# Both gates as one product of 2x2 blocks in seven block products, with sigmoids in DRAM and a merge stage of its own

## The chip, the cores and the metric

The kernel runs on one core of a Trainium2 chip. The metric is device microseconds of one execution; several runs are given by their median. The engines of the core work in parallel, each in the order of its own queue, and wait for one another by semaphores: PE (TensorE, matrix products and transposes), DVE (VectorE), ACT (ScalarE), POOL (GpSimd, which here also issues DMAs that store to DRAM) and SP (SyncE, which here issues the DMA loads).

## The reference

One decoder block on x of 1024 tokens and 1024 channels, all in float32. The part that matters here:

```python
h = rmsnorm(x, norm1_g[l])
proj = h @ w_in[l]
...
gate_a = jax.nn.sigmoid(proj[..., QKV_COLS + 2 * SGU_WIDTH:QKV_COLS + 2 * SGU_WIDTH + D_MODEL])
gate_b = jax.nn.sigmoid(proj[..., QKV_COLS + 2 * SGU_WIDTH + D_MODEL:])
...
sgu = spatial_gating(uv, sgu_ln_g[l], sgu_ln_b[l], w_spatial[l], b_spatial[l])

merged = gate_a * (attn @ w_proj_attn[l]) + gate_b * (sgu @ w_proj_sgu[l])
x = x + merged @ w_out[l]

h2 = rmsnorm(x, norm2_g[l])
ff = jax.nn.silu(h2 @ w_ffn_gate[l]) * (h2 @ w_ffn_up[l])
x = x + ff @ w_ffn_down[l]
```

Each gate is 1024 tokens x 1024 columns with 1024 summed; attn and sgu have 512 channels. `spatial_gating` applies Gelu to u and v, a layer norm to v, mixes v over 128 tokens with a triangular matrix for each of 8 groups, and multiplies by u.

## The kernel before

**Numbers.** A float32 matrix is kept as a pair of float32r: `split` (L102) writes the high part with a CAST on ACT (L103) and the rest with a subtraction on DVE (L104). A product of two such pairs is three matmuls (high x high, high x low, low x high), each 128 summed x 128 x 512 columns. H holds h, transposed, as 2 x 8 blocks of 128 channels x 1024 tokens.

**Stages.** RMSNorm to H; attention in four rounds (hp), whose result goes to DRAM as attd (tile tag "att", L588 to L593); the SGU stage with v and then u (eight token tiles T each, `rows_mm`, L363 to L365, Gelu L771); the gate stage (L818 on); the out product with W_o, which adds x (L1033); the FFN (`product`, L990 to L992, 22 column blocks); the down product; the last RMSNorm.

**The SGU's end.** After every second T of u, `mix` (products L739, and L743 on DVE with scalar_tensor_tensor) and `sgu_T` (four transposes for each T, L753, then four small splits of 128x128) are put into a table of slots: `at(slot, f)` runs f when PE's program has come to that slot, so the last ones fall among the gate products.

**The gate stage.** For ph 0 (gate_b and sgu) and ph 1 (gate_a and attention), for each of 8 column blocks c, and for each half of the tokens: `gate(half)` is 24 matmuls into "acc" (`cols_mm`, L376 to L378) and a Sigmoid (L828) into an SBUF tile "S"; `proj(half)` is 12 matmuls into "s", and DVE multiplies (L836; L838 and L839 add in ph 1) into the merged tile. In all 1152 matmuls. After the last column the 16 halves of merged are split into H.

**What sets the order.** Weights come through a queue of jobs: SP loads into a ring of three "raw" buffers, and `split_job` splits into a ring of 4096 columns, WH and WL. `combine_wd` (L807 to L812, one for each of 11 row pairs of w_ffn_down) forms differences of blocks on DVE for the down product; POOL loads (L801) and stores them (L812). A scheduler lays the program out, and each engine then runs its own instructions in the order laid down.

**The FFN's seven products.** With the four blocks of the weights b11, b21 (gate columns, lower and upper half of the sum) and b12, b22 (up columns), and of H (`OPS`; sums of blocks in HX), four results are made of seven block products instead of eight (Strassen and Winograd's form). `weights(f, i)` (L956 on) splits one block or a difference of blocks, five products ahead (AHEAD_W); `product(f, i)` multiplies.

## Time and profile before

| what | us |
|---|---|
| median of three runs (1715.13 to 1716.87) | 1716.21 |
| the profiled execution, its own time | 1713.07 |
| its span in the trace | 1711.4 |
| last product of u starts | 689.65 |
| first gate product starts | 690.02 |
| first add of x in the out stage | 964.62 |

The profile is of one execution. Its span runs from the first instruction to the last; some 1.7 us of the execution's time lie outside. A busy share is an average over stages with different limits, so the stage that is changed is read by its own windows. In a row of the timeline the first number is the start, the second the duration, then engine, line of the kernel, operation, out<-in; in brackets the engine's idle time before it and what ended that. An entry of the DMA list ends with the median time from issue to landing.

### The profile page before, as it was taken

The numbers are of one execution on the slowest core, as the hardware profiler recorded it, in microseconds if no ns is written. First come the engines' busy times: TensorE is split into PE (matmuls) and PEld (weight loads), VectorE is DVE, ScalarE is ACT, GpSimd is POOL, SyncE is SP. The second block draws the span as 40 slices with busy tenths as digits, with TensorE's granted clock in tenths as the row PEclk, the third lists the DMA queues.
The fourth block names the chain that finished last, engine by engine and source line by source line (L and its number), as shares of the span: only waits on it lengthen the run. The fifth ranks groups of instructions, "written<-read, shape, count | busy, mean of one in ns | idle before, by whom it ended". The sixth has DMA issues, their size and how long they took to land.

```text
span 1711.4 us, 22153 instructions
## 1 busy us (share of the span) xinstructions
PE 1679.3 (98%) x8206; PEld 1363.4 (80%) x8206; DVE 918.3 (54%) x1751; ACT 667.7 (39%) x1319; POOL 203.9 (12%) x361
## 2 busy tenths in 40 slices
PE   7999999999999999999999998999999999989998
PEld 7877877877887778888888886888888888778886
DVE  5355376357447655543323438565565555565555
ACT  5344435425434552311311226333333333354444
POOL 6200120030021124120000011010000000100003
PEclk9999999999999999999999998999999999999999
DMA  7312331152241215763311323233332332397563
GB/s 215 90 43 68 86 100 48 33 151 56 54 139 45 57 27 179 240 235 134 103 45 58 139 74 123 68 119 104 109 100 93 99 102 71 134 355 238 191 194 111
DMA packets 185740, 198.17 MB, mean 116 GB/s; under 512 B 13280, under 2 KB 140640, under 8 KB 185632
## 3 DMA queue, kind: packets, MB, share of 16 engines
q1 hardware_dynamic: 152656, 129.01, 24.3%
q0 software_dynamic: 17616, 58.31, 9.9%
q10 hardware_dynamic: 15360, 9.45, 2.3%
q8 instruction: 64, 1.05, 0.3%
q14 instruction: 44, 0.36, 0.1%
HBM read 144.84 MB, written 48.73 MB: 113 GB/s over the span
## 4 chain that ended last, share of the span: by engine, by line
PE 48%; issue 24%; POOL 2%; DVE 1%; DMA 1%; ACT 1%; SPq 0%; POOLq 0%; ACTq 0%; DVEq 0%
PE ps_acc L376 5%; PE ps_acc L377 5%; PE ps_acc L378 5%; PE ps_acc L364 4%; PE ps_acc L363 4%; PE ps_acc L365 4%; PE ps_dX L1116 2%; PE ps_dX L1117 2%; PE ps_dX L1118 2%; PE ps_s L377 2%; PE ps_s L378 2%; PE ps_s L376 2%; PE ps_s L463 2%; PE ps_dV L1118 1%; PE ps_dV L1116 1%
## 5 line engine op out<-in xcount | busy, mean ns | idle before, releaser
L103 ACT CAST WH<-raw 128x512 fp32r<-128x512 f32 (+2 forms) x179 | 138.5, 776 | 309.4 <-PE ps_acc L377 84.4
L376 PE MATMUL ps_acc<-H,WH 128*128 128x512 f32 x640 | 253.7, 396 | 0.0
L378 PE MATMUL ps_acc<-H,WL 128*128 128x512 f32 x640 | 253.2, 396 | 0.0
L377 PE MATMUL ps_acc<-H,WH 128*128 128x512 f32 x640 | 252.8, 395 | 0.0
L104 DVE TENSOR_TENSOR WL<-raw,WH 128x512 fp32r<-128x512 f32 (+2 forms) x179 | 157.0, 878 | 97.7 <-ACT WH L103 97.1
L363 PE MATMUL ps_acc<-WH,H 128*128 128x384 f32 (+1 forms) x512 | 190.9, 375 | 2.4 <-ACT H L103 2.4
L365 PE MATMUL ps_acc<-WH,H 128*128 128x384 f32 (+1 forms) x512 | 190.8, 373 | 0.5 <-DVE H L104 0.5
L364 PE MATMUL ps_acc<-WL,H 128*128 128x384 f32 (+1 forms) x512 | 189.2, 371 | 0.0
L376 PEld LDWEIGHTS ps_acc<-H,WH 128*128 128x128 f32 x640 | 120.2, 188 | 26.9 <-issue 1.2
L378 PEld LDWEIGHTS ps_acc<-H,WL 128*128 128x128 f32 x640 | 120.3, 188 | 26.8 <-issue 0.3
L377 PEld LDWEIGHTS ps_acc<-H,WH 128*128 128x128 f32 x640 | 120.2, 188 | 25.9 <-issue 0.5
L481 ACT ACTIVATE S<-S,sm 128x128 f32<-128x128 f32 (+1 forms) x192 | 84.9, 444 | 80.6 <-DVE sm L479 74.7
L363 PEld LDWEIGHTS ps_acc<-WH,H 128*128 128x128 f32 x512 | 97.1, 190 | 15.0 <-ACT H L103 2.9
L365 PEld LDWEIGHTS ps_acc<-WH,H 128*128 128x128 f32 x512 | 97.3, 190 | 12.8 <-issue 1.0
L364 PEld LDWEIGHTS ps_acc<-WL,H 128*128 128x128 f32 x512 | 96.8, 189 | 11.5 <-DVE WL L104 0.4
L990 PE MATMUL ps_X<-H,WH 128*128 128x512 f32 x264 | 104.5, 396 | 0.7 <-ACT sn L995 0.7
L991 PE MATMUL ps_X<-H,WH 128*128 128x512 f32 x264 | 104.5, 396 | 0.0
L992 PE MATMUL ps_X<-H,WL 128*128 128x512 f32 x264 | 101.0, 393 | 0.0
L104 DVE TENSOR_TENSOR WL<-rows,WH 128x512 fp32r<-128x512 f32 x66 | 45.4, 691 | 89.8 <-ACT WH L103 89.8
L103 ACT CAST WH<-rows 128x512 fp32r<-128x512 f32 x66 | 40.7, 622 | 129.9 <-PE ps_X L991 92.0
L104 DVE TENSOR_TENSOR WL<-ab,WH 128x512 fp32r<-128x512 f32 x74 | 51.1, 691 | 59.1 <-ACT WH L103 59.1
L103 ACT CAST WH<-ab 128x512 fp32r<-128x512 f32 x74 | 46.0, 621 | 76.3 <-PE ps_dV L1117 40.7
(292 smaller groups left out, 3240.7 us busy)
## 6 DMA issues: line engine op xcount, KB each, us to landing
raw<-in_w_in_dram SPq DMA_DIRECT2D x48, 512.0 KB
att<-in_w_ffn_down_dram POOLq DMA_DIRECT2D x22, 512.0 KB, 4.7
twd<-att POOLq DMA_DIRECT2D x22, 512.0 KB, 3.3
rows<-in_w_ffn_gate_dram SPq DMA_DIRECT2D x22, 512.0 KB
rows<-in_w_ffn_up_dram SPq DMA_DIRECT2D x22, 512.0 KB
ab<-twd SPq DMA_DIRECT2D x44, 256.0 KB
ab<-in_w_ffn_down_dram SPq DMA_DIRECT2D x30, 256.0 KB
raw<-in_w_in_dram SPq DMA_DIRECT2D x32, 192.0 KB
```

The costliest lines, as they stand in the source:

```text
L103: nc.scalar.copy(hi, src)
L104: return tt(out=lo, in0=src, in1=fb(hi), op=ALU.subtract)
L363: mm(o, H[:, 0, kt, tok], wh, start=(kt == 0), stop=False)
L364: mm(o, H[:, 0, kt, tok], wl, start=False, stop=False)
L365: mm(o, H[:, 1, kt, tok], wh, start=False, stop=(kt == KT - 1))
L376: mm(ps, WH[:, w], rh[:, half_of(half)], start=(kt == 0), stop=False)
L377: mm(ps, WH[:, w], rl[:, half_of(half)], start=False, stop=False)
L378: mm(ps, WL[:, w], rh[:, half_of(half)], start=False, stop=(kt == n - 1))
L481: nc.scalar.activation(sbt[:, o:o + n], sbt[:, o:o + n], AF.Exp, bias=neg[:, i:i + 1], scale=0.125, accum_out=stt[:, b, 2 + h:3 + h])
L990: mm(ps, WH[:, w], OPS[i](0, k), start=first and k == 0, stop=False, skip_group_check=True)
L991: mm(ps, WH[:, w], OPS[i](1, k), start=False, stop=False, skip_group_check=True)
L992: mm(ps, WL[:, w], OPS[i](0, k), start=False, stop=k == 3, skip_group_check=True)
```

## The change

The gate stage is replaced by two stages. In the first, gate_a and gate_b are one product of h with [gate_a | gate_b]: for each of 8 column blocks c, seven block products of 12 matmuls, with the functions `weights` and `product` that the FFN had (now made by `seven`, used by both). Their results are sigmoids of 128 x 1024, which POOL stores to gates_d. In the second, "merge", sgu and attention are loaded from DRAM (sgud, attd), split, multiplied by the projection weights, and multiplied by the sigmoids, loaded back from gates_d.

For the block sums of h, `combine_h1(T)` is called in u's T = 1 to 4 (for T - 1): eight adds on DVE and four stores of 256 KB to s7d. Before the gate stage the sums are loaded back and split into HX and into half of H. `sgu_T` no longer splits: one copy on ACT and one store to sgud. The table of slots is emptied before the gate stage (the loop over `sched`), and the pools of the first stages are closed, so nothing of the SGU runs among the gate products. `combine_wd` runs once for each c of the gate stage and three times in the merge. Splits are as before, but stand one line on (L104, L105), and so do other lines.

```diff
-            split(sguT[i][0][:, tok_of(T)], sguT[i][1][:, tok_of(T)], ps[:, i * P:(i + 1) * P])
+        t = T_("vst", [P, 4, P])
+        nc.scalar.copy(t.rearrange("p i t -> p (i t)"), ps)
+        nc.gpsimd.dma_start(out=sgud[:, :, tok_of(T)], in_=t)
...
+    def combine_h1(T):
+        a, b = tok_of(T), tok_of(T + 4)
+        x0, x1 = (T_("att", [P, 2, 4, P]) for _ in range(2))
+        for t, tok in ((x0, b), (x1, a)):
+            for j, kk in enumerate((LO, HI)):
+                tt(out=t[:, j], in0=fb(H[:, 0, kk, tok]), in1=fb(H[:, 1, kk, tok]), op=ALU.add)
+        tt(out=x0[:, 1], in0=x0[:, 0], in1=x0[:, 1], op=ALU.add)
+        tt(out=x0[:, 0], in0=x1[:, 0], in1=x0[:, 0], op=ALU.subtract)
+        tt(out=x1[:, 0], in0=x0[:, 1], in1=x1[:, 0], op=ALU.subtract)
+        tt(out=x1[:, 1], in0=x1[:, 1], in1=x1[:, 0], op=ALU.subtract)
+        for i, t in enumerate((x0, x1)):
+            for j in range(2):
+                nc.gpsimd.dma_start(out=s7d[i][j][:, :, a], in_=t[:, j])
...
+            if 1 <= T < 5:
+                combine_h1(T - 1)
...
+    for n in sorted(sched):
+        for f in sched.pop(n):
+            f()
+    close_pool(first_pool)
+    close_pool(first_psum)
...
+        def keep(f, i, src):
+            a = ring[0] % 8 * 512
+            ring[0] += 1
+            marks["lo"] = split(WH[:, a:a + 512], WL[:, a:a + 512], src)
+            slots[f, i] = a
+        def weights(f, i):
+            g, u = raw[f]
+            b11, b21, b12, b22 = flat(g[:, LO]), flat(g[:, HI]), flat(u[:, LO]), flat(u[:, HI])
+            if i in (1, 2, 3):
+                return keep(f, i, {1: b11, 2: b21, 3: b22}[i])
+            if i == 6:
+                t2 = T_("raw", [P, 512])
+                ts[f] = {5: b11, 6: t2, 7: b12, 4: b21}
+                for o, p, q in ((b11, b12, b11), (t2, b22, b11), (b12, b22, b12), (b21, b21, t2)):
+                    tt(out=o, in0=p, in1=q, op=ALU.subtract)
+            keep(f, i, ts[f][i])
...
+            ps, a = acc[f, b], slots.pop((f, i))
+            for k in range(4):
+                w = slice(a + k * P, a + (k + 1) * P)
+                mm(ps, WH[:, w], OPS[i](0, k), start=first and k == 0, stop=False, skip_group_check=True)
+                mm(ps, WH[:, w], OPS[i](1, k), start=False, stop=False, skip_group_check=True)
+                mm(ps, WL[:, w], OPS[i](0, k), start=False, stop=k == 3, skip_group_check=True)
+            if i in (1, 6, 7):
+                snap[f, i] = T_("sn", [P, 512])
+                nc.scalar.copy(snap[f, i], ps)
+            after(f, i, ps, acc.get((f, "V")), snap, f == nf - 1)
...
+    def gates_after(c, i, ps, V, snap, last):
+        sig = lambda o, src: nc.scalar.activation(o, src, AF.Sigmoid)
+        if i == 2:
+            o = go[c, 0] = T_("go", [P, S])
+            tt(out=o[:, t0], in0=snap.pop((c, 1)), in1=ps, op=ALU.add)
+            sig(o[:, t0], o[:, t0])
+        if i == 7:
+            o = go[c, 1] = T_("go", [P, S])
+            tt(out=o[:, t1], in0=snap.pop((c, 7)), in1=V, op=ALU.add)
+            sig(o[:, t1], o[:, t1])
+            if last:
+                tt(out=o[:, t0], in0=snap[c, 6], in1=V, op=ALU.add)
+            combine_wd(c)
+            load_wd(c + 1, "raw") if c + 1 < KT else None
+        if i == 4:
+            sig(go[c, 0][:, t1], ps)
+            put(gates_d[0][c], go.pop((c, 0)))
+        if i == 3:
+            o = go.pop((c, 1))
+            tt(out=o[:, t0], in0=o[:, t0] if last else snap[c, 6], in1=ps, op=ALU.add)
+            sig(o[:, t0], o[:, t0])
+            put(gates_d[1][c], o)
...
+    for n in range(5):
+        weights(*order[n])
+    with tc.issue_after(marks["load"].ins), tc.issue_after(marks["hi"].ins), tc.issue_after(marks["lo"].ins):
+        for i, j, dst in ((1, 0, 1), (0, 1, 0), (0, 0, None), (1, 1, 2)):
+            for q in range(2):
+                t = T_("raw", [P, 2, 512])
+                kk = slice(2 * q, 2 * q + 2)
+                nc.sync.dma_start(out=t, in_=s7d[i][j][:, kk])
+                if dst is None:
+                    split(H[:, 0, kk, t1], H[:, 1, kk, t1], t)
                 else:
-                    tt(out=sg, in0=sg, in1=pp, op=ALU.mult)
-                    tt(out=m, in0=m, in1=sg, op=ALU.add)
-
-            gate(0)
-            if late:
-                gate(1)
-                for i in range(NHP):
-                    need(("att", i))
-                proj(0)
-            else:
-                proj(0)
-                combine_wd(8 * ph + c - ph)
-                gate(1)
-            proj(1)
-        flags["sgu_dead"] = True
-    for half in range(2):
-        for c in range(KT):
-            merge_split(c, half)
-    close_pool(first_pool)
+                    split(HX[:, dst, 0, kk], HX[:, dst, 1, kk], t)
+    load_wd(0, "raw")
+    for n, (c, i) in enumerate(order):
+        if n + AHEAD_W < len(order):
+            weights(*order[n + AHEAD_W])
+        product(c, i)
+        if i == 7:
+            load_gates(c + 3)
...
+    sides = [[], []]
+    for side, src in enumerate(([sgud[:, i] for i in range(4)], attd)):
+        for i in range(4):
+            t = T_("raw", [P, S])
+            nc.sync.dma_start(out=t, in_=src[i])
+            pair = [T_(f"side{side}", [P, S], F32R) for _ in range(2)]
+            split(*pair, t)
+            sides[side].append(pair)
+        if side == 0:
+            stat["limit"] = len(jobs)
+            load_jobs()
+    load_wd(KT, "att")
+    sg = {}
+    def load_sg(c):
+        if c < KT:
+            sg[c] = [T_("sg", [P, S]) for _ in range(2)]
+            for j in range(2):
+                nc.sync.dma_start(out=sg[c][1 - j], in_=gates_d[1 - j][c])
+    load_sg(0)
+    for c in range(KT):
+        load_sg(c + 1)
+        m = T_("mg", [P, S])
+        for side in range(2):
+            for half in range(2):
+                pp = PS("acc")
+                cols_mm(pp, ("p", side, c), 4, lambda kt: sides[side][kt], half, half == 1)
+                gt, mh = sg[c][1 - side][:, half_of(half)], m[:, half_of(half)]
+                if side == 0:
+                    tt(out=mh, in0=gt, in1=pp, op=ALU.mult)
+                else:
+                    tt(out=gt, in0=gt, in1=pp, op=ALU.mult)
+                    tt(out=mh, in0=mh, in1=gt, op=ALU.add)
+                    split(H[:, 0, c, half_of(half)], H[:, 1, c, half_of(half)], mh)
+        if c in (1, 3, 5):
+            combine_wd(KT + c // 2)
+            load_wd(KT + c // 2 + 1, "att")
...
-            gate(0)
...
-                proj(0)
-                combine_wd(8 * ph + c - ph)
-                gate(1)
-            proj(1)
```

In the excerpts of the order below, an engine's instructions stand as it runs them: the line, the operation, the tiles (with the numbers of the build), the shape, and the semaphores that it waits for.

The first place is PE from u's last product to the first gate product. **Before** (L364, L365: u; ps_s<-A: mix(3); ps_acc_908: the first gate):

```order
L364 MATMUL ps_acc_899_6206<-WL_3_68,H_1_66 128x512
L365 MATMUL ps_acc_899_6206<-WH_2_67,H_1_66 128x512
L739 MATMUL ps_s_910_6302<-A_818_5574,pT_867_5894 128x128 [waits PE_49]
L376 MATMUL ps_acc_908_6288<-H_1_66,WH_2_67 128x512 [waits Activation_49]
L377 MATMUL ps_acc_908_6288<-H_1_66,WH_2_67 128x512
L739 MATMUL ps_s_910_6302<-A_818_5574,pT_867_5894 128x128 x2
L378 MATMUL ps_acc_908_6288<-H_1_66,WL_3_68 128x512 [waits DVE_49]
```

**After** (L719: mix(3); L733: the transposes of sgu_T(6) and sgu_T(7); ps_X_928: the first gate product):

```order
L346 MATMUL ps_acc_900_6227<-WH_2_67,H_1_66 128x512
L719 MATMUL ps_s_903_6261<-A_818_5579,cs_864_5893 128x128 [waits PE_49]
L719 MATMUL ps_s_903_6261<-A_818_5579,cs_864_5893 128x128 x3
L719 MATMUL ps_s_904_6270<-A_818_5579,cs_864_5893 128x128 [waits PE_49]
L719 MATMUL ps_s_904_6270<-A_818_5579,cs_864_5893 128x128 x3
L733 MATMUL ps_tr_905_6279<-ident_4_69,A_884_6074 128x128 [waits DVE_49,Activation_49]
...
L733 MATMUL ps_tr_905_6279<-ident_4_69,A_884_6074 128x128 [waits DVE_49]
L733 MATMUL ps_tr_907_6287<-ident_4_69,A_884_6074 128x128
L844 MATMUL ps_X_928_6407<-H_1_66,WH_2_67 128x512 [waits Activation_49]
L845 MATMUL ps_X_928_6407<-H_1_66,WH_2_67 128x512
L844 MATMUL ps_Y_931_6429<-H_1_66,WH_2_67 128x512 [waits Activation_49]
```

Where a gate product stood behind the first matmul of mix(3), all of mix(3) and the eight transposes now stand ahead of the first gate product, and the transposes wait for DVE.

The second place is DVE at the same point. **Before** (L743: mix(3); L104 with WL: weights; L104 with cs: low halves of sgu; L807: combine_wd):

```order
L743 SCALAR_TENSOR_TENSOR A_888_6052<-ps_s_910_6302,bsT_776_5304,A_888_6052 128x2x64 [waits PE_49]
L743 SCALAR_TENSOR_TENSOR A_888_6052<-ps_s_910_6302,bsT_776_5304,A_888_6052 128x2x64
L104 TENSOR_TENSOR WL_3_68<-raw_902_6238,WH_2_67 128x1024 [waits DMAHW7_49,Activation_49]
L743 SCALAR_TENSOR_TENSOR A_888_6052<-ps_s_910_6302,bsT_776_5304,A_888_6052 128x2x64 x2
L104 TENSOR_TENSOR cs_884_5998<-ps_tr_900_6210,oT_883_5997 128x128 [waits Activation_49]
L743 SCALAR_TENSOR_TENSOR A_888_6052<-ps_s_911_6311,bsT_776_5304,A_888_6052 128x2x64 [waits PE_49]
L743 SCALAR_TENSOR_TENSOR A_888_6052<-ps_s_911_6311,bsT_776_5304,A_888_6052 128x2x64 x3
L807 TENSOR_TENSOR att_937_6584<-att_937_6584 128x512 [waits DMASW6_49,DMASW0_49]
```

**After** (att_890 and att_891: combine_h1(3); L723: mix(3); gr_912: weights of the gates):

```order
L747 TENSOR_TENSOR att_891_6128<-H_1_66 128x512 [waits DMASW3_49,DMASW2_49]
L747 TENSOR_TENSOR att_891_6128<-H_1_66 128x512
L723 SCALAR_TENSOR_TENSOR A_884_6074<-ps_s_903_6261,bsT_776_5304,A_884_6074 128x2x64 [waits PE_49,Activation_49]
L723 SCALAR_TENSOR_TENSOR A_884_6074<-ps_s_903_6261,bsT_776_5304,A_884_6074 128x2x64 x3
L749 TENSOR_TENSOR att_890_6127<-att_891_6128,att_890_6127 128x512 [waits DVE_49]
L723 SCALAR_TENSOR_TENSOR A_884_6074<-ps_s_904_6270,bsT_776_5304,A_884_6074 128x2x64 [waits PE_49]
L723 SCALAR_TENSOR_TENSOR A_884_6074<-ps_s_904_6270,bsT_776_5304,A_884_6074 128x2x64 x3
L750 TENSOR_TENSOR att_891_6128<-att_890_6127,att_891_6128 128x512 [waits DVE_49]
L751 TENSOR_TENSOR att_891_6128<-att_891_6128 128x512 [waits DVE_49]
L105 TENSOR_TENSOR WL_3_68<-gr_912_6347,WH_2_67 128x512 [waits DMAHW3_49,Activation_49]
```

The adds of combine_h1(3) have come in ahead of mix(3) and between its two parts, and their first ones wait for stores (DMASW). Further on in the same queue **after** (HX: block sums of h; raw_926 and raw_927: load_wd's pair; raw_930: the difference of weights of which product (0, 6) is made):

```order
L105 TENSOR_TENSOR HX_909_6338<-raw_924_6393,HX_909_6338 128x1024 [waits DMAHW7_49,Activation_49]
L105 TENSOR_TENSOR WL_3_68<-gr_915_6352,WH_2_67 128x512 [waits PE_49,Activation_49]
L105 TENSOR_TENSOR HX_909_6338<-raw_925_6397,HX_909_6338 128x1024 [waits DMAHW0_49,Activation_49]
L871 TENSOR_TENSOR raw_926_6401<-raw_926_6401 128x512 [waits DMASW4_49,DVE_49]
L831 TENSOR_TENSOR raw_930_6422<-gr_913_6348,gr_912_6347 128x512 [waits DVE_49]
L831 TENSOR_TENSOR gr_912_6347<-gr_912_6347,raw_930_6422 128x512 [waits DVE_49]
L872 TENSOR_TENSOR raw_926_6401<-raw_927_6402,raw_926_6401 128x512 [waits DMASW5_49]
L105 TENSOR_TENSOR WL_3_68<-raw_930_6422,WH_2_67 128x512 [waits Activation_49]
```

The difference stands behind the last block sum and behind the first operation of combine_wd.

The third place is SP's queue of loads at the end of the gate products. **Before**, in the middle of the stage where ph 1 begins (in_w_in: gate weights; in_w_proj: projection weights; attd: attention):

```order
L136 DMA raw_953_6734<-in_w_proj_sgu_dram 128x4x128 [waits DMAHW7_49,DVE_49]
L136 DMA raw_961_6816<-in_w_in_dram 128x8x128 [waits DMAHW0_49,DVE_49]
L136 DMA raw_970_6912<-attd0_81 128x1024 [waits DMASW3_49,DMAHW1_49,DMASW2_49,DVE_49]
L136 DMA raw_973_6922<-attd1_82 128x1024 [waits DMASW7_49,DMAHW2_49,DMASW6_49,DVE_49]
L136 DMA raw_981_7013<-attd2_83 128x1024 [waits DMASW3_49,DMAHW3_49,DMASW2_49,DVE_49]
L136 DMA raw_995_7131<-attd3_84 128x1024 [waits DMASW4_49,DMAHW4_49,DMASW3_49,DVE_49]
L136 DMA raw_998_7140<-in_w_proj_attn_dram 128x4x128 [waits DMAHW5_49,DVE_49]
```

**After** (gr: the last gate weights; sgud: the sgu pieces; gate0_0 to gate1_1: the first four sigmoid tiles):

```order
L889 DMA gr_993_7059<-in_w_in_dram 128x8x128 [waits DMAHW4_49,DVE_49]
L949 DMA raw_1025_7486<-sgud_5306 128x1024 [waits DMASW4_49,DMASW3_49,DMASW5_49,DMASW1_49,DVE_49]
L949 DMA raw_1028_7492<-sgud_5306 128x1024 [waits DMASW5_49,DMASW4_49,DMASW6_49,DMASW2_49,DMASW7_49,DMASW1_49,DMASW0_49]
L949 DMA raw_1031_7498<-sgud_5306 128x1024 [waits DMASW6_49,DMAHW5_49,DMASW3_49,DMASW0_49]
L963 DMA sg_1055_7545<-gate1_0_6305 128x1024 [waits DMAHW0_49,DMASW7_49,DMAHW6_49,DMASW2_49,Activation_49]
L963 DMA sg_1054_7544<-gate0_0_6297 128x1024 [waits DMAHW7_49,DMAHW1_49,DVE_49]
L963 DMA sg_1057_7549<-gate1_1_6306 128x1024
L963 DMA sg_1056_7548<-gate0_1_6298 128x1024
L949 DMA raw_1034_7504<-sgud_5306 128x1024 [waits DMAHW3_49,DMAHW2_49,DVE_49]
L137 DMA raw_1037_7510<-in_w_proj_sgu_dram 128x4x128 [waits DMAHW4_49,DVE_49]
```

The loads of attention stood among gate weights whose products went on; now the first loads of the merge follow the last gate weights, and four sigmoid tiles stand ahead of the fourth sgu piece and of the first projection weights.

More of the change, by code (lines that the diff above doesn't have):

```diff
@@ L793, in hybrid_block @@
+    gates_d = [[dram.tile([P, S], F32, name=f"gate{j}_{c}") for c in range(KT)] for j in range(2)]
     NP = NF // 2
@@ new lines, in hybrid_block @@
+    weights, product = seven(KT, raw_g, gates_after)
+    order = seven_order(KT)
+    for c in range(3):
+        load_gates(c)
+    for n in range(5):
[8 more added lines that the diff above has]
+                    split(H[:, 0, kk, t1], H[:, 1, kk, t1], t)
+                else:
+                    split(HX[:, dst, 0, kk], HX[:, dst, 1, kk], t)
```

229 lines of the change are left out of this document (91 added, 138 removed).

## The prediction

> **What bounds the kernel now.** First the page's busy shares, then the windows view over the stage that the change rewrites.
>
> ```profile
> span 1711.4 us, 22153 instructions
> PE 1679.3 (98%) x8206; PEld 1363.4 (80%) x8206; DVE 918.3 (54%) x1751; ACT 667.7 (39%) x1319; POOL 203.9 (12%) x361
> ...
> 692.00:697.00 5.00, 5.00 (x29) 4.29 (x28) 3.35 (x8) 2.23 (x5) 1.07 (x2) 1.00 1.09 302
> 703.00:955.00 252.00, 252.00 (x1106) 207.29 (x1105) 95.34 (x134) 56.79 (x85) 16.52 (x31) 1.00 0.37 121
> 955.00:965.00 10.00, 10.00 (x45) 8.24 (x44) 3.64 (x6) 1.68 (x2) 0.11 (x1) 1.00 0.82 261
> ```
>
> A window's numbers are its length, then the busy time of PE, PEld, DVE, ACT and POOL, the granted clock, the DMA share and GB/s. PE is busy in all of 692 to 965 us at clock 1.00, across both ends of the gate stage, while DVE has 95 us of work in 252. So the stage is as long as its matmuls; one matmul less is a period less, and any wait that PE gets is added in full.
>
> The period comes from the timeline:
>
> ```profile
> 689.65 0.39 PE L365 MATMUL ps_acc<-WH,H 128*128 128x512 f32 x1
> 689.88 0.38 PE L739 MATMUL ps_s<-A,pT 128*128 128x128 f32 x2
> 690.02 0.48 PE L376 MATMUL ps_acc<-H,WH 128*128 128x512 f32 x1
> ...
> 829.78 0.39 PE L377 MATMUL ps_acc<-H,WH 128*128 128x512 f32 x1
> ...
> 834.77 0.39 PE L378 MATMUL ps_acc<-H,WL 128*128 128x512 f32 x1
> ```
>
> The last two rows start 4.99 us and 22 matmuls apart: 0.2268 us each. The first three show today's first joint: u's last product, the first two matmuls of mix(3), and the first gate product 0.14 us later. The gate matmuls stand around mix(3) and the sgu transposes, so nobody waits for those.
>
> **What the change removes.** A column pair of both gates takes 2 x 2 x 24 = 96 matmuls, as seven block products 7 x 12 = 84. Eight pairs save 96 matmuls, and the 384 of the projections stay: 96 x 0.2268 = **21.8 us** gained, on PE's path. ACT and DVE lose the 32 small sgu splits and the 16 final ones become 16 spread over the merge; these never bounded. The long middle of the stage can be judged by the FFN, which runs the same seven products:
>
> ```profile
> 1100.00:1480.00 380.00, 380.00 (x1650) 309.38 (x1649) 223.94 (x353) 134.76 (x237) 27.21 (x50) 1.00 0.31 101
> ```
>
> PE has no idle time there with DVE at 59%. A pair of gates takes PE 19.05 us (84 x 0.2268), and DVE 18 operations of 128x512 (seven lows, four differences, three gate sums, four for the down weights) at the 0.69 us of the rows below, 12.4 us: hidden too, if nothing is late at its start.
>
> **What it adds: two joints.** The puts and loads of the sigmoids (16 each, 512 KB) lie beside the matmuls at a DMA share of 0.37, and the gate weights wait only for buffers of the attention, so inside the stage neither costs anything; their price is at its ends. Before, the stages overlapped; now the seven-product stage needs sums of four blocks of h, which go through DRAM, and the merge needs sgu, attention and sigmoids back from DRAM.
>
> ```profile
> 665.88 2.16 DVE L743 SCALAR_TENSOR_TENSOR A<-ps_s,bsT,A 128x128 f32<-128x128 f32 x8 [2.66 <-PE ps_s L739]
> ...
> L104 DVE TENSOR_TENSOR WL<-rows,WH 128x512 fp32r<-128x512 f32 x66 | 45.4, 691 | 89.8 <-ACT WH L103 89.8
> ...
> L104 DVE TENSOR_TENSOR WL<-raw,WH 128x1024 fp32r<-128x1024 f32 x56 | 68.2, 1220 | 43.2 <-ACT WH L103 42.8
> ...
> L103 ACT CAST WH<-rows 128x512 fp32r<-128x512 f32 x66 | 40.7, 622 | 129.9 <-PE ps_X L991 92.0 <-PE ps_Y L991 34.7 <-PE ps_V L991 1.5
> ...
> L103 ACT CAST WH<-raw 128x1024 fp32r<-128x1024 f32 x56 | 58.5, 1051 | 117.9 <-PE ps_acc L365 46.8 <-PE ps_acc L377 33.5 <-PE ps_s L377 13.5
> ...
> L995 ACT COPY sn<-ps_X 128x512 f32<-128x512 f32 x66 | 36.5, 583 | 5.5 <-PE ps_X L992 5.5
> ...
> att<-in_w_ffn_down_dram POOLq DMA_DIRECT2D x22, 512.0 KB, 4.7
> twd<-att POOLq DMA_DIRECT2D x22, 512.0 KB, 3.3
> ...
> x2d<-rows POOLq DMA_DIRECT2D x8, 512.0 KB, 3.0
> ...
> L812 POOL DMA_DIRECT2D twd<-att x22 | 11.8, 538 | 71.6 <-DVE att L808 51.3 <-DVE att L810 14.2 <-DVE qkr L104 6.1
> ...
> 623.43 0.83 POOL L762 DMA_DIRECT2D S<-in_w_spatial_dram  x1 [5.79 <-issue]
> ...
> 628.30 1.04 POOL L707 TENSOR_SCALAR_AFFINE_SELECT S<-S 128x128 f32<-128x128 f32 x4 [4.04 <-DMA S<-in_w_spatial_dram]
> ```
>
> The first row and the last two are of the timeline, the six with a bar are groups (their count; busy us, mean ns of one), the three of POOLq are of the DMA issues (their count, KB each, us from issue to landing).
>
> *u to gates, PE's first wait.* combine_h1 puts 4 x 8 adds of 0.69 us (5.5 us per T) into DVE's queue, and two "att" buffers make each T wait for the puts of the one before. Such a put (256 KB in runs of 512 bytes) is bounded by the last two rows, a load of that shape: 0.83 us to issue, 4.04 until it is seen. Chained from 668.1, where mix(1) ends (665.88 + 2.16), T1 ends near 679.6, T2 near 688.7, and T3 starts near 691. DVE's order shows mix(3)'s last eight scalar-tensor-tensors behind T3's adds, so they end at about 697.5. u's last product ends at 689.9 as before; 1.6 us of mix(3) and transposes are all PE still has, until 691.5. The transposes wait for DVE; then come two ACT copies (0.58 each, the COPY row), the first weight CAST (0.62) and the first product: 697.5 + 0.5 + 1.2 + 0.6 = 699.8. PE waits **8.3 us**. The low end, with DVE on time (693): 4 us.
>
> *u to gates, second wait.* After 699.8 PE has only eight products before (0,6), the first that needs a difference of weights: 96 x 0.2268 = 21.8 us, to 721.6. In front of that difference DVE has in its order 15 x 0.69 (weight lows, differences, one gate sum), 8 x 1.22 (lows of the reloaded blocks) and 8 x 0.69: 25.7 us, and its reloads come through three "raw" buffers. The last puts of T3 leave at about 700 and land at 704 to 706; eight 512 KB loads, each 3.0 us (the x2d row) and then 1.05 on ACT and 1.22 on DVE before its buffer is free, through three buffers: 5.3 / 3 = 1.8 us apiece, 14 us more. The difference takes its "raw" buffer behind these and behind load_wd's pair (4.7 us, the row of att<-in_w_ffn_down), and is made at about 727.3. (0,6) starts near 728, and (1,6), whose difference waits for the ring once more, ends near 736.6. With 8.3 us already lost it should have been 718.7 without either wait: **17.9 us** for the joint. Ends: 12 (DVE on time, loads of 3 us side by side) and 24 (each put at its 0.83 + 4.04 in series, each ring turn at its full latency).
>
> *Gates to merge.* The other end of the stage is bounded by these rows:
>
> ```profile
> L828 ACT ACTIVATE S<-ps_acc 128x512 f32<-128x512 f32 x32 | 19.1, 597 | 98.2 <-PE ps_acc L378 93.4 <-DVE A L836 4.7
> ...
> 959.01 4.56 SPq L879 DMA_DIRECT2D rows<-in_x_dram  x8
> ...
> 964.62 0.69 DVE L1033 TENSOR_TENSOR rows<-rows,ps_acc 128x512 f32<-128x512 f32 x1 [5.71 <-DMA rows<-in_x_dram]
> ...
> 967.00:969.00 2.00, 2.00 (x11) 1.65 (x10) 0.38 (x1) 0.00 (x0) 0.00 (x0) 1.00 1.02 418
> ```
>
> SP works through its queue in order. In it the load of the first sigmoid tile (sg<-gate1_0) writes where the last sigmoids lie, so it waits until the last put of gates_d has landed: after the last gate matmul a sigmoid (0.60), the issue (0.54) and 3.3 us, 4.4 in all. Behind it stand three more sigmoid tiles, then the fourth sgu piece, then the projection weights. A burst of eight 512 KB loads is in the trace: full DMA share and 418 GB/s, 1.3 us apiece, but 5.6 us from issue to the first user. So five pieces are there after 8 to 9.5 us, 14 us after the last gate matmul; a CAST of 1.05 and the weights' CAST of 0.62 follow, and the first merge product starts at 16. Then the attention pieces come through the same three buffers. PE has 56 matmuls (12.7 us) that need none; it gets the first product with attention at about 30.8. Loss: 30.8 - 12.7 = 18.1, taken as **18 us**. Ends: 11 (every piece as quick as a single 512 KB load) and 22 (the weights also at 3.3 each behind it).
>
> *The clock.* The trace has one long wait of PE:
>
> ```profile
> 1050.00:1060.00 10.00, 4.23 (x15) 3.24 (x16) 10.00 (x17) 7.56 (x14) 2.38 (x3) 0.51 0.31 105
> ...
> 1058.00 1.12 PE L214 MATMUL ps_tr<-ident,raw 128*128 128x128 f32 x4 [4.29 <-ACT rows L218]
> ...
> 1059.35 0.63 PE L991 MATMUL ps_X<-H,WH 128*128 128x512 f32 x1
> ...
> 1063.19 0.63 PE L991 MATMUL ps_X<-H,WH 128*128 128x512 f32 x1
> ...
> 1063.98 0.39 PE L990 MATMUL ps_Y<-H,WH 128*128 128x512 f32 x1
> ```
>
> After 4.29 us of idling the granted clock is 0.51; ten of the matmuls, 1059.35 to 1063.19 with nine periods, come 0.427 apart, and 1063.98 on at 0.227: twelve slow ones in all before that row, 12 x 0.2 = 2.4 us. The change makes four such waits. Most of these 2.4 us lie ahead of PE's next wait and vanish in it; I take **1 us**.
>
> The Trainium skill (TensorE: Matmul & The Clock Gate, Part 1: The HAM clock gate) says the same of the array clock: a window without work halves it, and the first 3.4 us or so of renewed work run at half rate. That speaks against a change that pays for fewer matmuls with idle windows: by the rule each of the four waits is followed by its slow stretch, four times 2.4 us instead of my 1, and the sum is 1740, the third rival below. The trace agrees on the halving (0.51), and cannot show whether a slow stretch that lies between two waits costs anything.
>
> *The merge's end.* The split of column c now follows its sum at once, so the out stage finds 14 of 16 pieces ready; before, PE did not wait there either (955 to 965). Nothing.
>
> **Sum.** -21.8 + 17.9 + 18 + 1 = +15.1 us. Against the profiled execution (1713.07 us, span 1711.4) that is 1728.2; the median shown is 1716.21, 3.1 above it, so I forecast **1731 us**.
>
> **Rivals.**
> 1. *Faster: the sigmoid load does not hold up SP.* If its buffer has come free earlier than the last put (the semaphore's count, not the tile, decides), the fourth sgu piece and the weights land before the gate stage ends and only the attention pieces are late, about 4 us; with the first joint at its low end, 12, the sum is -21.8 + 12 + 4 = -5.8: **1710**. It decides where both joints together fall under 21.8 us. For it: three sgu pieces stand ahead of that load and nothing else in SP's queue needs the last put; DMA share is 0.37 in the stage, so transfers have room. Against: PE's own last products lie 4.4 us ahead of that landing, and DVE's order at the first joint is fixed. 0.15.
> 2. *No change: both joints near their low ends*, 12 + 11 - 21.8 = +1.2 to +2: **1718**. For it: latencies of 3 us, not bursts. 0.10.
> 3. *Clock on top:* the four waits each keep their 2.4 us, +9.6 in place of +1: **1740**. For it: the row at 1058. Against: where DVE or DMA sets the next start, slow matmuls cost nothing. 0.15.
> 4. *DVE never catches up:* were each low to wait for its CAST (7 x 0.62) and each pair for the load of the down weights (4.7), DVE's pair would take 12.4 + 4.3 + 4.7 = 21.4 us, 2.4 over PE's, 16 over the last seven pairs less what the first joint already counts: 1745. Against: the FFN's 380 us without a wait. 0.05.
>
> The forecast itself, with 3 to 25 us of loss, 0.55.
>
> **Range and chances.** The bounds of both joints give -21.8 + 23 = +1.2 and -21.8 + 46 + 1 = +25; ends of the same sign at both places are less likely than mixed ones, so 1710 (rival 1) to 1741. A run can tell 0.2% (3.4 us) from no change: faster 0.15, same 0.10, slower 0.75.
>
> **What would show it.** Right: 96 PE matmuls fewer; PE idle twice at the first joint, first with the release by DVE's scalar-tensor-tensor and the sgu transposes, then by the CAST of a weight difference at (0,6); twice at the second, with DMA as releaser of the first CASTs, SP's sigmoid load released by the gates_d put; no PE idle between (2,6) and (7,4). Wrong: (0,6) without a wait; merge products within 5 us of the last gate product; idle time of PE inside the later pairs; or the attention pieces ready when the sgu half is done.

## The result and the profile after

| | before | after |
|---|---|---|
| median of four runs, us | 1716.54 (1715.13 to 1717.78) | 1730.82 (1730.62 to 1736.87) |
| ratio to before, 95% interval | | 1.0092 [1.0069, 1.0115] |
| profiled execution, its span, us | 1711.4 | 1729.3 |
| u's last product starts | 689.65 | 690.72 |
| last matmul of gates and projections starts | 955.3 | 976.0 |
| first FFN product starts | 1058.77 | 1080.95 |
| last product of the FFN, of the down stage starts | 1488.83, 1703.51 | 1509.59, 1720.05 |

The kernel is slower by 14.3 us in the medians and by 17.9 in the two spans. The page and the windows of the changed kernel (columns as in the prediction):

```profile
span 1729.3 us, 22340 instructions
PE 1666.9 (96%) x8110; PEld 1349.4 (78%) x8110; DVE 999.2 (58%) x1860; ACT 704.4 (41%) x1371; POOL 229.9 (13%) x401
...
690.00:701.00 11.00, 5.38 (x30) 3.83 (x30) 7.88 (x18) 2.41 (x5) 5.82 (x10) 0.79 0.60 168
...
726.00:731.00 5.00, 0.66 (x2) 0.40 (x2) 3.94 (x6) 1.98 (x3) 0.40 (x1) 0.95 0.53 175
...
760.00:860.00 100.00, 100.00 (x438) 81.85 (x437) 53.67 (x85) 39.55 (x69) 17.46 (x33) 1.00 0.64 221
...
873.00:882.00 9.00, 0.00 (x0) 0.00 (x0) 2.77 (x4) 0.00 (x0) 1.08 (x2) 0.50 1.03 407
```

PE has 96 matmuls fewer (8206 to 8110), and the middle of the new stage is full. PE stands still at both joints; in the last row neither PE nor ACT runs anything and DVE is busy for 2.8 of 9 us, while the DMAs run at their full share. PE's waits in its timeline:

```profile
696.57 1.11 PE L733 MATMUL ps_tr<-ident,A 128*128 128x128 f32 x4 [3.68 <-DVE A L723]
698.12 1.21 PE L733 MATMUL ps_tr<-ident,A 128*128 128x128 f32 x4 [0.43 <-DVE A L723]
700.84 0.80 PE L844 MATMUL ps_X<-H,WH 128*128 128x512 f32 x1 [1.51 <-ACT WH L104]
...
730.34 0.69 PE L844 MATMUL ps_X<-HX,WH 128*128 128x512 f32 x1 [4.67 <-ACT WH L104]
...
864.70 0.50 PE L844 MATMUL ps_X<-H,WH 128*128 128x512 f32 x1 [0.68 <-ACT sn L849]
...
867.33 0.39 PE L846 MATMUL ps_X<-H,WL 128*128 128x512 f32 x1
883.74 0.79 PE L357 MATMUL ps_acc<-side,WH 128*128 128x512 f32 x1 [16.02 <-ACT WH L104]
...
893.54 0.73 PE L357 MATMUL ps_acc<-side,WH 128*128 128x512 f32 x2 [1.27 <-ACT side L104]
```

5.6 us of waits ahead of the first gate product, 4.7 ahead of (0,6) and 1.7 in four small ones behind it, 17.3 in the merge: 29.9 us with the 0.7 at 864.70, where PE waits for ACT's copy of a result (a snapshot, "sn"). The kernel before has no wait of 0.25 us or more from 560 to 1010 us. What ended them stands on the other engines of the same execution, first at u to gates (DVE), then at gates to merge (SP, ACT):

```profile
692.14 1.29 DVE L747 TENSOR_TENSOR att<-H 128x512 f32<-128x512 f32 x2 [1.68 <-DMA s7d<-att]
...
697.46 1.12 DVE L723 SCALAR_TENSOR_TENSOR A<-ps_s,bsT,A 128x128 f32<-128x128 f32 x4
...
726.79 1.22 DVE L105 TENSOR_TENSOR HX<-raw,HX 128x1024 fp32r<-128x1024 f32 x1 [0.62 <-ACT HX L104]
728.34 0.69 DVE L871 TENSOR_TENSOR raw<-raw 128x512 f32<-128x512 f32 x1 [0.33 <-DMA raw<-in_w_ffn_down_dram]
728.95 0.68 DVE L831 TENSOR_TENSOR raw<-gr,gr 128x512 f32<-128x512 f32 x1
```

```profile
870.73 1.85 SPq L963 DMA_DIRECT2D sg<-gate  x4
872.70 0.53 SPq L949 DMA_DIRECT2D raw<-sgud  x1
...
882.12 1.04 ACT L104 CAST side<-raw 128x1024 fp32r<-128x1024 f32 x1 [10.95 <-DMA raw<-sgud]
```

mix(3) ends at 698.6, behind adds that waited for stores; the difference for (0,6) is made at 729.6, behind the last reload and the first operation of the down pair. The fourth sgu piece is issued at 872.7 and there only at 882.1, behind four sigmoid tiles and beside a pair of down weights, at 407 GB/s.

### The profile page after: what moved, and what is told of

Read it like the earlier page. It is cut to its first block, busy times and chain, and to the rows that moved or that the text cites. A ratio compares the mean times of both kernels' runs of the same rounds, so it can differ in the third digit from the quotient of the medians.

```text
span 1729.3 us, 22340 instructions
## 1 busy us (share of the span) xinstructions
PE 1666.9 (96%) x8110; PEld 1349.4 (78%) x8110; DVE 999.2 (58%) x1860; ACT 704.4 (41%) x1371; POOL 229.9 (13%) x401
## 4 chain that ended last, share of the span: by engine, by line
PE 39%; issue 26%; DMA 6%; DVE 3%; POOL 3%; ACT 1%; SPq 0%; POOLq 0%; ACTq 0%; DVEq 0%
PE ps_acc L345 3%; PE ps_acc L344 3%; PE ps_acc L346 3%; PE ps_acc L357 3%; PE ps_acc L359 3%; PE ps_acc L358 3%; PE ps_dX L1193 2%; PE ps_dX L1194 2%; PE ps_dX L1195 2%; PE ps_s L444 2%; PE ps_X L844 1%; PE ps_X L846 1%; PE ps_X L845 1%; DMA att<-in_w_ffn_down_dram 1%; PE ps_dV L1195 1%
## 5 line engine op out<-in xcount | busy, mean ns | idle before, releaser
L105 DVE TENSOR_TENSOR WL<-rows,WH 128x512 fp32r<-128x512 f32 x132 | 91.1, 692 | 133.2 <-ACT WH L104 133.2
L104 ACT CAST WH<-rows 128x512 fp32r<-128x512 f32 x132 | 81.8, 621 | 207.6 <-PE ps_X L845 102.8
L104 ACT CAST WH<-raw 128x512 fp32r<-128x512 f32 (+2 forms) x105 | 85.3, 817 | 171.8 <-PE ps_V L845 53.1
L357 PE MATMUL ps_acc<-H,WH 128*128 128x512 f32 x384 | 154.0, 401 | 0.0
L359 PE MATMUL ps_acc<-H,WL 128*128 128x512 f32 x384 | 153.9, 401 | 0.0
L358 PE MATMUL ps_acc<-H,WH 128*128 128x512 f32 x384 | 153.3, 399 | 0.0
L844 PE MATMUL ps_X<-H,WH 128*128 128x512 f32 x360 | 143.3, 398 | 2.9 <-ACT WH L104 1.5
L845 PE MATMUL ps_X<-H,WH 128*128 128x512 f32 x360 | 142.8, 397 | 0.0
L105 DVE TENSOR_TENSOR WL<-raw,WH 128x512 fp32r<-128x512 f32 (+2 forms) x105 | 97.2, 930 | 41.4 <-ACT WH L104 41.1
L845 PE MATMUL ps_V<-HX,WH 128*128 128x512 f32 x232 | 91.0, 393 | 0.0
L844 PE MATMUL ps_V<-HX,WH 128*128 128x512 f32 x232 | 91.0, 393 | 0.0
L846 PE MATMUL ps_V<-HX,WL 128*128 128x512 f32 x232 | 90.8, 392 | 0.0
L359 PEld LDWEIGHTS ps_acc<-H,WL 128*128 128x128 f32 x384 | 72.6, 189 | 16.5 <-issue 0.3
L105 DVE TENSOR_TENSOR WL<-ab,WH 128x512 fp32r<-128x512 f32 x74 | 51.1, 690 | 59.3 <-ACT WH L104 59.3
```

Of the source, the lines that this page charges most:

```text
L104: marks["hi"] = nc.scalar.copy(hi, src)
L105: return tt(out=lo, in0=src, in1=fb(hi), op=ALU.subtract)
L357: mm(ps, WH[:, w], rh[:, half_of(half)], start=(kt == 0), stop=False)
L358: mm(ps, WH[:, w], rl[:, half_of(half)], start=False, stop=False)
L359: mm(ps, WL[:, w], rh[:, half_of(half)], start=False, stop=(kt == n - 1))
L844: mm(ps, WH[:, w], OPS[i](0, k), start=first and k == 0, stop=False, skip_group_check=True)
```

## The experiments

All but e7 were timed in several runs beside the kernel before (1715.2 to 1715.9 in these jobs). Each also has a profile of one execution, and a stretch is read from the starts in PE's timeline ("u ends" is the start of u's last product): from u's last product to the first gate product, on to the last gate product, and from that to the last merge product. The first row is the changed kernel.

| run | time, us | ratio to before | u ends | to first gate | to last gate | merge stretch |
|---|---|---|---|---|---|---|
| after | 1730.82 | 1.0092 [1.0069, 1.0115] | 690.7 | 10.1 | 166.5 | 108.7 |
| e1 | 1733.75 | 1.0105 [1.0090, 1.0120] | 689.6 | 9.9 | 167.6 | 110.3 |
| e2 | 1731.71 | 1.0085 [1.0071, 1.0100] | 692.9 | 10.9 | 164.4 | 109.4 |
| e3 | 1730.71 | 1.0084 [1.0070, 1.0098] | 694.3 | 5.7 | 166.4 | 110.8 |
| e4 | 1735.84 | 1.0113 [1.0099, 1.0127] | 693.5 | 10.9 | 167.5 | 108.8 |
| e5 | 1731.94 | 1.0091 [1.0077, 1.0105] | 691.9 | 10.4 | 168.5 | 107.2 |
| e6 | 1728.13 | 1.0070 [1.0054, 1.0086] | 692.7 | 5.7 | 160.8 | 109.5 |
| e7 (e1 again) | 1736.2, one run | | 693.1 | 10.1 | 168.6 | 109.4 |
| e8 | 1718.40 | 1.0015 [1.0005, 1.0026] | 694.3 | 5.7 | 159.2 | 101.2 |
| e9 | 1718.81 | 1.0026 [1.0015, 1.0037] | 693.1 | 5.7 | 160.7 | 103.9 |
| e10 | 1718.39 | 1.0021 [1.0012, 1.0030] | 694.4 | 5.7 | 161.1 | 103.6 |
| e11 | 1717.89 | 1.0016 [1.0006, 1.0027] | 694.5 | 5.7 | 162.6 | 101.2 |
| e12 | 1715.92 | 0.9998 [0.9990, 1.0007] | 690.8 | 5.7 | 163.6 | 103.8 |

A caution for all of them: after, e1, e2, e4, e5 and e7 run the same work up to u's end and reach it between 689.6 and 693.5 us, and the merge, which is the same in after, e2, e3, e4 and e6 but for e4's extra matmuls, takes 108.7 to 110.8. e8 and e10 turned out to be one program built twice, and so did e9 and e11; their merges differ by 2.4 and 2.7 us. So one stretch of one profile is good to some 3 us, and u's end to some 4.

### e1 and e7: the sigmoids behind what PE needs first

```diff
-    load_sg(0)
+    with tc.issue_after(behind[0]), tc.issue_after(behind[1]):   # 4th sgu piece, 2nd projection weights
+        load_sg(0)
+        load_sg(1)
     for c in range(KT):
-        load_sg(c + 1)
+        if c:
+            load_sg(c + 1)
```

> Edit: on SP the loads of the first four sigmoid tiles stand behind the fourth sgu piece and the first projection weights; nothing else moves. Theory T (transfers ahead of the piece that PE needs set the second joint): of the 9 us in which all engines idled at 407 GB/s, four tiles of 512 KB, 2 MB, go away ahead of the fourth piece: PE's wait of 16.0 us at the first merge product falls to 8 to 10 us, the time falls by 6 to 8 us against the changed kernel, to 1723 to 1725. Rival L (the landing of the last sigmoid store and the row of CASTs set it): the wait stays above 14 us and the time within 2 us of 1730.8. Rival B (all of the 2 MB is needed soon anyway): the first wait falls, but the wait for the attention pieces grows from 1.3 us by as much, and the time stays.

PE's waits in e1's merge:

```profile
878.34 0.80 PE L357 MATMUL ps_acc<-side,WH 128*128 128x512 f32 x1 [10.92 <-ACT WH L104]
...
891.02 0.74 PE L357 MATMUL ps_acc<-side,WH 128*128 128x512 f32 x2 [3.20 <-ACT side L104]
...
903.71 0.50 PE L358 MATMUL ps_acc<-side,WH 128*128 128x512 f32 x1 [1.46 <-DVE side L105]
```

The first wait fell by 5.1 us, so the order does set it; but 5.8 us of waits follow where 1.3 did (the larger ones are shown), and the stretch is no shorter. That is rival B: the bytes were put off, not away. The same kernel was run again:

> The kernel of e1 once more, for one look: whether its first wait of 10.9 us and its later waits of 5.8 us in the merge, and the stretch of 110.3 us from the last gate product to the last merge product, come again. Theory T and rival B both expect the same within 1.5 us; where the stretch falls under 107 us, the loss seen in e1 was a chance of the clock's slow stretches.

It holds e1's edit alone. The waits came again (10.6 us the first, 15.8 in all) and so did the stretch, 109.4: no chance of the clock.

### e5: fewer bytes, the order as it was

```diff
-    load_wd(KT, "att")
...
-        if c in (1, 3, 5):
-            combine_wd(KT + c // 2)
-            load_wd(KT + c // 2 + 1, "att")
+        if c in (2, 4, 6):
+            with tc.issue_after(marks["sg"].ins):
+                load_wd(KT - 1 + c // 2, "att", nc.sync)
+        if c in (3, 5, 7):
+            combine_wd(KT + c // 2 - 1)
```

> Edit: the last three pairs for the down weights, which the merge loads on POOL as soon as it begins, are loaded on SP behind the sigmoid tiles of columns 3, 5 and 7. Theory T (the second joint is as long as the bytes that are moved ahead of what PE needs, at some 400 GB/s): 1 MB less ahead of the fourth sgu piece makes PE's wait of 16.0 us 13 to 14, another 1 MB of loads and 1 MB of stores less makes the wait for the attention pieces (1.3 us) go; the stretch from the last gate product to the last merge product, 108.7 us, becomes 105 to 106; the time falls by 2 to 4 us against 1730.8. Rival L (latency, not bytes): wait and stretch stay within 1 us.

The first wait became 11.2 us, shorter than the 13 to 14 that were forecast, and a new one of 3.1 us came at 902.5; the stretch is 1.5 us shorter, no more than two profiles of one program differ by, and the time did not move. Order alone and bytes alone gave next to nothing.

### e2, e3 and e6: the two limits of the first joint

e2 forms the differences without a buffer of their own, e3 moves the calls for the block sums:

```diff
-                t2 = T_("raw", [P, 512])
...
+                    tt(out=b12, in0=b22, in1=b12, op=ALU.subtract)
+                    tt(out=t2, in0=b12, in1=b11, op=ALU.add)          # t2 is b11
+                    tt(out=b21, in0=b21, in1=t2, op=ALU.subtract)
...
+            if i == 5 and nf == KT:
+                tt(out=b11, in0=b22, in1=b11, op=ALU.subtract)
```

```diff
             if which == 1:
                 ln(T)
+                if T % 2:
+                    combine_h1(T // 2)
                 continue
...
-            if 1 <= T < 5:
-                combine_h1(T - 1)
```

> Edit: the gates' weight differences are formed in the four blocks themselves (the difference for product 5 only after that for product 6 was split), so that none needs a raw buffer. Theory Q (the difference for (0,6) is late because its buffer comes from the ring behind the eight reloads and the pair for the down weights): PE's wait of 4.7 us ahead of (0,6) and the small ones behind it, 6.3 us together, fall to 2 or less, and the time falls by 4 to 5 us, to 1726 to 1727. Rival R (the reloaded block sums themselves are as late as the difference): another wait of 3 to 5 us appears within the next three products, at one that reads a reloaded block, and the time falls by less than 2 us.

The waits at (0,6) are gone, and 2.1 us of the stretch; but the weights' buffers come free later, and PE waits 2.5 us at 767 for a load of weights (in DVE's timeline the next difference waits 9.3 us for it) and 1.9 us at 795. Of the 4 to 5 us the time shows none.

> Edit: the four calls that form block sums of h are made in the loop over v, one for every second tile, not in that over u. Theory D (DVE is late at the first joint because those adds, paced by their stores, are queued ahead of mix(3), and the reloads wait for the last of these stores): PE's waits of 4.1 and 1.5 us ahead of the first gate product go to 1 to 2 together, the reloads start some 15 us sooner, (0,6) waits at most 1 us; the time falls by 9 to 12 us, to 1719 to 1722. Rival S (DVE has no room beside the attention either, 64% busy there): PE gets new waits of 5 us or more between 575 and 690 us and the time falls by less than 5 us.

In this run the first gate product follows u's end by 5.7 us instead of 10.1, as theory D says. The time did not move, where 9 to 12 us were forecast: u's last product comes 3.6 us later in this profile, within the spread of u's end, and (0,6) starts late all the same, with nothing of DVE's adds left ahead of it:

```profile
699.94 0.50 PE L844 MATMUL ps_X<-H,WH 128*128 128x512 f32 x1 [1.61 <-ACT WH L104]
727.99 0.80 PE L844 MATMUL ps_X<-HX,WH 128*128 128x512 f32 x1 [5.68 <-ACT WH L104]
```

Three reloads now stand ready in the raw ring, but the other five, the down pair and the difference still take their turns in it after 700. So there are two limits, one behind the other. Both taken away:

> Edit: e2 and e3 together. Theory Q2 (the first joint has two limits one behind the other, DVE's adds ahead of mix(3) and the ring of raw buffers that serves eight reloads, the down pair and the difference; each edit alone leaves the other): no wait of 4 to 6 us ahead of (0,6) any more and 1.5 us instead of 5.6 ahead of the first gate product; from u's last product to the last gate product 176.6 us become 168 to 170; the time falls by 4 to 7 us against 1730.8, less what the adds cost in v. Rival K (the sum of PE's waits stays, as reloaded blocks are next late, and the clock's slow stretches take the rest): over 173 us.

166.4 us from u's end to the last gate product instead of 176.6: more than e2's and e3's shares added (1.3 and 4.5), as Q2 has it; e8 to e11, which hold both edits too, have 164.9 to 168.3. Here (0,6) starts at 714.92 without a wait. The profiled execution, with a span of 1720.9 us, keeps 8.4 us of it. It is the fastest of six, which spread from 1722.6 to 1730.9; their median keeps 2.7, less than the 4 to 7 that were forecast. What spreads them was not settled.

### e4: the clock

```diff
+    pd = PS("acc")
+    for n in range(64):
+        mm(pd, H[:, 0, 0, :P], H[:, 0, 1, :512], start=n == 0, stop=n == 63, skip_group_check=True)
     load_sg(0)
```

> Edit: 64 extra matmuls, read by nobody, between the last gate product and the first merge product, 14.6 us in a wait of 16.0. Theory A (the slow clock after that wait is absorbed by PE's next wait, for the attention pieces): the first merge products come 0.229 us apart instead of 0.427, the next wait grows from 1.3 us by the 1.9 us gained, and the time stays within 0.7 us of 1730.8. Rival C (each slow stretch costs its own time): the time falls by 1.5 to 2.4 us. If the extra matmuls delay the first merge product, the trace shows it by a start later than 16 us after the last gate product.

PE was kept at work through the wait (clock 1.00 from 873 to 888 us, against 0.50 in the window above), and the first merge product still came 16.4 us after the last gate product. But the slow stretch was only moved. The first row is a window of the changed kernel, the second one of e4:

```profile
883.74:887.50 3.76, 3.76 (x9) 2.98 (x10) 1.89 (x3) 0.65 (x2) 1.07 (x2) 0.50 1.02 343
...
889.90:893.30 3.40, 3.40 (x9) 2.63 (x8) 0.92 (x2) 0.62 (x1) 0.95 (x2) 0.50 0.96 306
```

In e4 the first products run at full clock, and 1.7 us later PE works at half clock about as long as in the changed kernel (3.4 us against 3.8). So the equal stretches of the merge, 108.8 and 108.7 us, decide nothing between theory A and rival C: the slow clock wasn't taken away. For theory A speaks the trace of the changed kernel alone, in which PE's next wait, 1.27 us at 893.54, is ended by a CAST that itself waited for a DMA:

```profile
892.45 1.04 ACT L104 CAST side<-raw 128x1024 fp32r<-128x1024 f32 x1 [2.22 <-DMA raw<-attd]
```

Faster products would have waited longer there. That is an argument, not a test. The time is 5 us longer, but 4.6 us of that stand in this profile before the last gate product, where the two programs have the same instructions in the same order on every engine; why this build is slower there stays open.

### e8 to e12: all together, and what was left

> Edit: e1, e2, e3 and e5 together. Theory T: with the pairs gone, the order of e1 pays: PE's first wait of the merge is 8 to 9 us, later ones 3 us together, the stretch from the last gate product to the last merge product 101 to 104 us; with the first joint as in e6 the time is 1717 to 1722, still not under the kernel before. Rival B (the bytes needed before PE can go on are as many in any order): the stretch stays over 106 us and the time over 1723.

```profile
868.36 0.79 PE L357 MATMUL ps_acc<-side,WH 128*128 128x512 f32 x1 [8.75 <-ACT WH L104]
877.95 0.51 PE L358 MATMUL ps_acc<-side,WH 128*128 128x512 f32 x1 [0.53 <-DVE side L105]
```

These are all of PE's waits in e8's merge of a quarter us and more. With e1's order and e5's bytes together the stretch is 7.5 us shorter here and 5.1 in e10, the same program built again, where they gave nothing and 1.5 alone. The median is 1718.4 us, 12.4 less than the changed kernel and 9.7 less than e6, which lacks these two edits. (The profiled execution was the fastest of twelve.)

> Edit: e8, and in front of the sgu pieces on SP the first projection weights, split while the last gate products run. Theory T2 (in e8 PE waits 9.1 us at the second joint although three sgu pieces are there, because its first weights stand behind the fourth piece): the wait between the last gate product and the first merge product becomes 2 to 3 us; PE then gets six matmuls from each piece and waits some 4 to 6 us in parts; the stretch from the last gate product to the last merge product, 101.2 us, becomes 96 to 98; time 1713 to 1716 (e8: 1718.4). Rival L2 (the fourth piece and the attention pieces come no sooner, and PE uses up what it has): the stretch stays above 100 us.

```diff
     sides = [[], []]
+    stat["limit"], stat["at"] = stat["load"] + 1, ring[0] % 8 * 512
+    load_jobs()
+    split_job()
```

The first merge product now follows the last gate product by 2.0 us, as forecast, but PE waits 11.7 us in all, 7.2 of them for the first attention piece. The stretch is 103.9, and in e11, which has the same order, 101.2; e8 and e10 have 101.2 and 103.6. That is rival L2: the first product comes 7 us sooner and the last one no sooner. What comes last is the data. The time, 1718.81 us, missed the 1713 to 1716 of theory T2.

> Edit: e8 with the block sums made in v's tiles 4 to 7 instead of 1, 3, 5, 7. Theory V (in e8 the sums take DVE from the attention's softmax between 584 and 600 us: PE's four waits there, 2.9 us of them and the slow clock that follows): those waits go; u's last product ends 2 to 3 us sooner than in e8; time 1715 to 1717. Rival W (the sums run into mix(3) again or into the last attention round): the wait ahead of the first gate product grows from 1.6 us to over 3, or PE waits between 640 and 690 us; time as e8 or more.

> Edit: e9 and e10 together. If both theories hold, the gains add: from u's last product to the last merge product 260 to 262 us (before: 265.7, e8: 266.1), and the time is 1710 to 1713, under the kernel before by 3 to 5 us. If rival L2 or W holds, 1714 or more.

```diff
-                if T % 2:
-                    combine_h1(T // 2)
+                if T >= 4:
+                    combine_h1(T - 4)
```

The edit moved nothing: every engine of e10 has the instructions of e8 in the order of e8 (the first store of the sums is issued at 509 to 510 us in both), and e11 those of e9. They are the same programs built twice; the times of the first two, 1718.40 and 1718.39, agree. Neither tested theory V, and e11's 1717.89 us is above the 1710 to 1713 that both theories together forecast. So the calls were tied to the layer norm, on top of e9:

```diff
+                if T >= 4:
+                    with tc.issue_after(marks["ln"].ins):
+                        combine_h1(T - 4)
```

> Edit: e9, but each call of the block sums is tied behind the layer norm of v's tile 4, 5, 6 or 7 on DVE's queue. In e8, e9, e10 and e11 the scheduler put the sums at the same places of DVE's queue, from about 570 us on, wherever the call stood, so e10 moved nothing. Theory V, tried in earnest: PE's four waits between 560 and 601 us, 2.6 us, go, and u's last product ends at 690 to 692 us (e9: 693.1); the first gate product is not later than 6 us after u's last product; the time is 1714 to 1716.5. Rival W: the sums reach into mix(3) or the last attention round, the wait ahead of the first gate product grows to over 3 us, and the time stays at 1718 or more.

The stores now run from 629.7 to 664.5 us, the four waits between 560 and 601 us are gone, u ends at 690.8 (692.7 to 694.5 in the six runs with the sums earlier in v), and the first gate product follows it no later. The median is 1715.92 us, a ratio of 0.9998 [0.9990, 1.0007]. Theory V holds for the waits and for u's end, and the time is in its range, 2.8 us under the median of all 20 runs of e9 and e11. That the one comes from the other is less sure: in the profiles e12 gains 2.3 us against e9 up to u's end and loses 2.8 again among the gate products, where PE waits 3.4 us at 786.53 behind late loads of weights. This is the best version found, and it equals the kernel before; none was faster.

## Why the prediction was right, point by point

**The mechanism was right; that 1731 us met the median of 1730.82 so closely was luck.** Against the profiled executions the forecast was 1728.2 for 1730.99, and there the joints came out larger than forecast and the down stage won back most of that. The remaining 2.8 us were made up by adding the 3.1 us by which the profiled execution of before lay under its median; that of the changed kernel lies on its median.

**The gain, 21.8 us,** stood in full: 96 matmuls are gone, and the stretch between the joints is full.

**The first joint, 17.9 us.** The mechanism was right at each step: adds paced by stores ahead of mix(3) (its end was forecast at 697.5, it came at 698.6), first product 699.8 (700.84), difference 727.3 (made by 729.6), (0,6) near 728 (730.34). e3 and e6 showed that it takes both limits to make the joint. Measured, u's end to the last gate product is 176.6 us; less 672 matmuls of 0.2268 (152.4), mix(3) and the transposes (about 3.4) and the snapshot's wait (0.7) leaves 20.1. But these aren't all waits, as the prediction had it: PE waits 5.6 us (8.3 forecast) and then 6.3 (9.6); 4.6 us are starts more than 0.33 us apart without a wait, most of them at half clock, and 3.6 are spread over the rest.

**The second joint, 18 us.** Again the steps hold: SP's sigmoid loads released by a store (3.0 us after the last gate product ended, forecast 4.4), the fourth piece 14.4 us after it (14), the first merge product 16.0 (16). The store was the last but one, which landed at 870.67; the last one landed at 872.96, when SP had gone on. Behind that two errors cancelled. The first product with attention came at 891.07, 23.4 us after the last gate product ended, not at 30.8; but only 24 matmuls (5.4 us) stood ahead of it in PE's order, not 56 (12.7 us). 23.4 - 5.4 is 18.0 again. What the term left out follows: the second attention piece, used 25.8 us after, brought the wait of 1.27 us, and more came in small delays. The stretch of 108.7 us less 384 x 0.2268 = 87.1 leaves 21.6; 17.3 us of that are waits, and starts more than 0.33 us apart without a wait add 3.0. What set the wait was bytes as much as order; the prediction named the queue's order, which e1 shows not to be enough.

**The clock, 1 us,** can't be told apart from the joints in the sum. PE worked at half clock behind the first gate product, behind (0,6) and behind the first merge product; the fourth of the forecast waits, 1.27 us long, was followed by none:

```profile
700.84:706.50 5.66, 5.66 (x13) 4.47 (x14) 5.59 (x9) 2.12 (x4) 1.66 (x3) 0.50 0.95 246
730.50:733.90 3.40, 3.08 (x7) 1.97 (x8) 3.40 (x6) 0.88 (x2) 0.55 (x1) 0.50 0.91 293
883.74:887.50 3.76, 3.76 (x9) 2.98 (x10) 1.89 (x3) 0.65 (x2) 1.07 (x2) 0.50 1.02 343
```

Half of these 12.8 us, an estimated 6.4, is the price before any of it vanishes in a wait. The first stretch lies ahead of the wait for (0,6), which the reloads, the down pair and their CASTs set on DVE, and the last ahead of the wait for the attention piece, so most of it should vanish, as the prediction argued. No run shows how much: e4 was made for that and only moved the slow stretch. The third rival's 1740 us did not come about. The Trainium skill's rule (TensorE: Matmul & The Clock Gate, Part 1: The HAM clock gate) would have each wait of some 3.4 us or more followed by its slow stretch; the trace agrees that the clock halves, at 0.50. Whether that price reaches the end stays open.

**Beyond the joints** the prediction had nothing, and there was something. The out stage reaches the FFN 1.5 us later still. The FFN, and above all the down stage, then win time back: 214.5 us from first to last product of the down stage before, 210.2 after and in all twelve experiments, since two waits are gone that the kernel before has (its timeline):

```profile
1502.10 1.20 PE L1116 MATMUL ps_dX<-WH,H 128*128 128x512 f32 x4 [2.01 <-ACT WH L103]
...
1506.76 1.20 PE L1116 MATMUL ps_dX<-WH,H 128*128 128x512 f32 x4 [1.64 <-ACT WH L103]
```

Why they go was not tried. In sum: +1.1 until u's end, -21.8 + 20.1 + 21.6 + 0.7 in the stretch, less 1.0 by which the stretch of before itself exceeds its matmuls, mix(3) and transposes, is +20.7 at the last merge product; +1.5 to the FFN, -1.4 in it, -4.2 in the down stage and +1.4 at the end make 17.9, but for rounding.

**The rivals.** The first (SP not held up) and the second (both joints at their low ends) did not occur; nor did the fourth: PE has no wait of 0.25 us or more between 744 and 864 us, inside the later pairs.

## What to carry to other kernels

A product that needs fewer multiplications but its operands in another form is paid for at its ends: price the reload, in bytes at the measured rate of a burst, against the work that is ready meanwhile, before counting the matmuls saved. When a joint has two limits one behind the other, taking one away shows little in the stretch and nothing in the time; judge an experiment by the stretch it should shorten, and then take both away. And look at the order that the scheduler made before believing that an edit moved anything.
